# Seven products for eight in a quarter of the DeltaNet's v and z projections

## The chip, the cores and the metric

The kernel runs on one core of a Trainium2 chip, as one launch. The metric is the device time of that launch in microseconds, the median of several runs. TensorE multiplies matrices (its result lands in PSUM), VectorE (DVE in the profile) and ScalarE (ACT) do the elementwise work, GpSimd (POOL) some small work, and SyncE (SP) issues nearly all DMAs.

## The reference

Two decoder layers over 256 tokens of width 2048, all in float32: an attention layer (MLA) and a gated DeltaNet layer, each followed by a SwiGLU feed-forward and an embedding gate. The change is in the DeltaNet:

```python
proj = hn @ w_in                       # 256 x 2048 times 2048 x 12352
qkv, z, b, a = split(proj, ...)        # q 2048, k 2048, v 4096, z 4096, b 32, a 32 columns
qkv = silu(causal_depthwise_conv(qkv, conv_w))
...
o = chunk_gated_delta_rule(q, k, v, g, beta)     # from q, k, v; 32 heads
o = rms_norm(o, out_norm) * silu(z)
return o @ w_out
```

So z is needed late (when a head group's output is gated) and v when a head group is scanned, while q and k of all heads come first, because a triangular inverse over all heads is made from them.

## The kernel before

**Products.** Every float32 product is made of three TensorE passes on rounded operands: with x = xh + xl and w = wh + wl it sums xh·wh, xh·wl and xl·wh (lines 312 to 314, in `products`). Weights come in as raw tiles of four k-tiles by 512 columns (`wload`, a DMA of 1 MB on SyncE's queue) and are cut in two by `wsplit`: ScalarE casts `wh` (line 110), VectorE subtracts to get `wl` (line 111). There are 3 tiles each of `raw`, `wh` and `wl`, taken in turn; in the feed-forward stages `EXTRA` adds 3, 1 and 1.

**Plain projections.** `linear` takes blocks of 512 columns. A block is 16 k-tiles by two halves of 128 tokens by three passes, so 96 matmuls of 512 columns, which are summed in two PSUM banks and then copied out by the block's `evac`.

**Seven products for eight.** `seven` takes two column blocks at once. For part of the k-tiles it treats tokens, k and columns as a 2 x 2 by 2 x 2 block product and makes it with seven half-size products in place of eight (Strassen's scheme in Winograd's form). With `s` = 2 the first four k-tiles are treated so, in seven `phase`s of two k-tiles each (6 matmuls); the remaining k-tiles go as usual. The weight operands of those phases are sums and differences of raw blocks, made by VectorE in place (lines 344, 351, 358, 369), and each has to be split by `wsplit` again. The operands on the side of the tokens come from a `Half` object: eight transposes, `xf`, its split `xh`, `xl`, four sums `f`, and their split. `seven` waits for that object in its first phase: `op` calls `until`, which advances queued work until it is there. The feed-forward stages of both layers use `seven`, the DeltaNet does not.

**Queued work.** Work of another kind is written as generators in two lists, `fill` and `back`. `tick` advances the first generator of each list by one step, and `linear` and `seven` call it after every six matmuls. So the order in which instructions are written comes from these calls; a scheduler then settles each engine's order when the kernel is built, and each engine works through its own in that order.

**The DeltaNet stage.** First the four q and the four k projections, in pairs b = 0 to 3; `queries(b)` and `keys(b)` are queued behind them. `queries` convolves (`conv`: transposes, a scaled copy on ScalarE, twelve multiply-adds on VectorE, Silu) and sums squares with TensorE (`tr<-ones,sq`). `keys` convolves and then runs `group` for two head groups: products of `kap` and `rho` on TensorE, `dg`/`ssk` on VectorE, a power and a scaling of `E` on GpSimd, `LT` and `AT` on VectorE, then their stores. The eighth and last group is number 7. Behind q and k come eight z blocks, and after the first of them `fill` is emptied and `lanes` (62 small VectorE steps) is queued. One v block follows; then, with `scan(gg)` of eight head groups queued, the other seven v blocks and the output projection `w_out`.

The code that the change touches is this:

Of the kernel before, what the change touches and what calls it, by code (L numbers as in the profile page):

```python
# [11 lines left out]
F32R = mybir.dt.float32r  # L12
BF16 = mybir.dt.bfloat16
I32 = mybir.dt.int32
AF = mybir.ActivationFunctionType
# [5 lines left out]
P = 128  # L21
T = 2
# [16 lines left out]
Y2 = 3  # L39
S4 = 21  # L40
WBUFS = {"raw": 3, "wh": 3, "wl": 3}
EXTRA = {"raw": 3, "wh": 1, "wl": 1}
OGY = 5
PRE = 1
SY = 2
KY = 3
NV0 = 1
P2 = {"mla": 13, "gdn": 8, "ffn": 2, "ple": 2}


def cody_waite():
# [12 lines left out]
def trunk(ctx: ExitStack, tc: tile.TileContext, a: dict, out, plan=("mla", "ffn", "ple", "gdn", "ffn", "ple"), first=0):  # L64
# [25 lines left out]

    def wtile(kind, dt):

        more = EXTRA[kind] if scope.get("extra") is not None else 0
# [24 lines left out]
    nc.vector.memset(neghalf, -0.5)  # L118
    ones = const.tile([P, P], F32, name="ones")
    nc.vector.memset(ones, 1.0)  # L120

    def rsqrt_(t, n):
        nc.gpsimd.tensor_tensor(out=t, in0=t, in1=neghalf[:, :n], op=ALU.pow)  # L123
# [165 lines left out]
            assert fill or back  # L289
            tick()  # L290

    def linear(xs, W, kt, blocks, evac, row0=0, need=None, step=4):

        for bi, (c0, n) in enumerate(blocks):
            ps = [psmm.tile([P, 512], F32, tag="mm", name="mm") for _ in range(T)]
            for k4 in range(0, kt, 4):
                kn = min(4, kt - k4)
                raw = wload(W, row0 + k4 * P, c0, kn, n)
                wh, wl = wsplit(raw, kn, n, step)
                for kk in range(kn):  # L300
                    k = k4 + kk
                    if need is not None:
                        need(k // 4)
                    until(lambda: len(xs) > k // 4)
                    for t in range(T):
                        products(ps[t], part(xs, k, t), wh, wl, kk, n, k == 0, k == kt - 1)
                    tick()
            evac(bi, c0, n, ps)

# [467 lines left out]
    def gdn(j, nrm, nxt, mc, ctx):  # L777
# [88 lines left out]
        def project(c0):  # L866
# [7 lines left out]
            linear(nrm.x, W, 16, [(c0, 512)], evac)  # L874
            return xs

        def conv(acc, xs, f0):
            for pair in range(2):
                tr = trp()
                for k2 in range(2):  # L880
                    for t in range(T):
                        o = k2 * 256 + t * P
                        kk = pair * 2 + k2
                        nc.tensor.transpose(out=tr[:, o:o + P], in_=xs[:, t, kk * P:(kk + 1) * P], identity=ident)
                for k2 in range(2):
                    f = f0 + pair * 2 + k2
                    o = (pair * 2 + k2) * 256
                    src = tr[:, k2 * 256:(k2 + 1) * 256]
                    scaled(acc[:, o:o + 256], src, cw[:, 3 * 64 + f:3 * 64 + f + 1])
# [204 lines left out]
                yield from group(2 * b + i, rho, kap, Es[i])  # L1094

        lane_pool = tc.tile_pool(name="lane", bufs=1)
        with lane_pool as lp, tc.tile_pool(name="p2a", bufs=1) as scope["p2"]:
            for b in range(4):
                rho, Es = p4("rho"), []
                fill.append(queries(b, project(b * 512), rho, Es))  # L1100
                fill.append(keys(b, project(2048 + b * 512), rho, Es))
            for gg in range(8):
                linear(nrm.x, W, 16, [(8192 + gg * 512, 512 if gg < 7 else 256)],
                       lambda bi, c0, n, ps, gg=gg: gate_z(gg, 0, n, ps))
                if gg == 0:
                    while fill:
                        tick()
                    back.append(lanes(lp))
            first_v = [project(4096 + gg * 512) for gg in range(NV0)]
            while back:  # L1110
                tick()
        build = ctx.enter_context(tc.tile_pool(name="build", bufs=1))
        scope["p2"] = ctx.enter_context(tc.tile_pool(name="p2c", bufs=P2["gdn"]))
        tts = [build.tile([P, 8, P], F32, name=f"tt{i}") for i in range(2)]
        dd = build.tile([P, 8, 64], F32, name="dd")
        for z in (*tts, dd):
# [134 lines left out]
    for n, (s, i) in enumerate(steps):  # L1251
        last = n == len(steps) - 1
        nxt = None if last else Norm(WC[kind[steps[n + 1][0]], steps[n + 1][1]], {"ffn": 4}.get(steps[n + 1][0]))
        with ExitStack() as ctx:
            mc = ctx.enter_context(tc.tile_pool(name=f"{s}{n}", bufs=1))
            scope["extra"] = mc if s == "ffn" else None
# [41 lines left out]
```

## Time and profile before

| what | value |
|---|---|
| median of three runs | 2789.31 us (2788.46 to 2790.66) |
| the profiled execution's own time | 2787.68 us |
| span of its instructions | 2785.9 us |
| TensorE busy with matmuls | 2748.1 us, 13537 matmul records |
| VectorE busy | 2074.4 us |
| ScalarE busy | 1508.1 us |

The span is counted from the first to the last instruction of the profiled execution; 1.8 us of its time lie around it. Busy times of engines overlap, so they are not to be added. A matmul's recorded duration includes its way through the array and overlaps with the next one's; the distance between two starts says what a matmul costs in a row.

### The profile page before, as it was taken

The page shows a single profiled execution, that of the slowest core. Times are in us where ns is not written, and L with a number is a line of the kernel's source. Part 1 is how long each engine was busy: PE and PEld are TensorE (multiplying, and loading weights), DVE is VectorE, ACT ScalarE, POOL GpSimd, SP SyncE. Part 2 cuts the span into 40 slices and gives each one's busy share as a digit, 9 for nine tenths or more (in the row PEclk, how much of TensorE's full clock was granted, in tenths as well). Part 3 has the DMA queues.
Part 4 walks back from the last instruction along what each step waited for, and adds up shares of the span by engine and source line. Part 5 has one row for each costly group of instructions (what it writes and reads, how often), then busy time and mean ns, then how long its engine had stood idle before and what let it go on. Part 6 is the DMA issues. An engine that isn't in the chain of part 4 may idle for free.

```text
span 2785.9 us, 33751 instructions
## 1 busy us (share of the span) xinstructions
PE 2748.1 (99%) x13537; PEld 2281.5 (82%) x13537; DVE 2074.4 (74%) x1990; ACT 1508.1 (54%) x1625; POOL 170.5 (6%) x256
## 2 busy tenths in 40 slices
PE   8999999999999999999999999999999999999999
PEld 8888888888888888778888888888888888888887
DVE  5776888988978765566684556657898988989764
ACT  6765655655555555654444444444665655555553
POOL 1430000000000000233200000000000000000000
PEclk9999999999999999999999999999999999999999
DMA  7436465655566645666677545556565555655544
GB/s 226 129 119 206 150 240 181 226 172 201 186 211 212 221 134 174 215 218 225 225 263 248 198 156 188 165 172 217 181 215 192 186 193 182 239 205 204 192 155 141
DMA packets 296445, 540.81 MB, mean 194 GB/s; under 512 B 34105, under 2 KB 55266, under 8 KB 296034
## 3 DMA queue, kind: packets, MB, share of 16 engines
q1 hardware_dynamic: 295698, 536.52, 56.7%
q8 instruction: 106, 1.74, 0.3%
q10 hardware_dynamic: 592, 2.15, 0.2%
q14 instruction: 49, 0.40, 0.0%
HBM read 517.63 MB, written 21.00 MB: 193 GB/s over the span
## 4 chain that ended last, share of the span: by engine, by line
PE 89%; DVE 4%; ACT 3%; POOL 2%; issue 1%; DMA 1%; SPq 0%; DVEq 0%; POOLq 0%; ACTq 0%
PE mm L312 28%; PE mm L314 28%; PE mm L313 27%; DVE wl L111 2%; PE tr L156 1%; PE tr L1041 1%; ACT wh L110 1%; PE tr L1151 1%; PE tr L1157 1%; DMA E<-Gd 1%; POOL E L927 1%; ACT junk L178 1%; POOL r L123 0%; PE tr L944 0%; DVE kvs L582 0%
## 5 line engine op out<-in xcount | busy, mean ns | idle before, releaser
L111 DVE TENSOR_TENSOR wl<-raw,wh 128x2048 fp32r<-128x2048 f32 (+4 forms) x618 | 1265.2, 2062 | 436.7 <-ACT wh L110 435.6
L110 ACT CAST wh<-raw 128x2048 fp32r<-128x2048 f32 (+4 forms) x618 | 1059.2, 1725 | 832.8 <-PE mm L314 639.2
L312 PE MATMUL mm<-wh,xh 128*128 128x512 f32 (+3 forms) x3576 | 1407.8, 394 | 1.1 <-ACT xh L165 0.7
L314 PE MATMUL mm<-wh,xl 128*128 128x512 f32 (+3 forms) x3576 | 1385.2, 388 | 0.0
L313 PE MATMUL mm<-wl,xh 128*128 128x512 f32 (+3 forms) x3576 | 1383.0, 387 | 0.5 <-DVE wl L111 0.5
L314 PEld LDWEIGHTS mm<-wh,xl 128*128 128x128 f32 x3576 | 673.3, 188 | 137.4 <-DVE xl L654 0.2
L312 PEld LDWEIGHTS mm<-wh,xh 128*128 128x128 f32 x3576 | 674.3, 189 | 134.7 <-ACT u L354 3.8
L313 PEld LDWEIGHTS mm<-wl,xh 128*128 128x128 f32 x3576 | 674.5, 189 | 132.5 <-DVE wl L111 3.9
L123 POOL TENSOR_TENSOR re<-re,neghalf 128x2 f32<-128x2 f32 x2 | 5.4, 2722 | 1333.4 <-DVE re L748 1333.4
L344 DVE TENSOR_TENSOR raw<-raw 128x2048 f32<-128x2048 f32 (+1 forms) x34 | 65.0, 1911 | 14.2 <-DMA raw<-in_ffn_w_down 7.2
L702 ACT ACTIVATE sg<-mm,rs 128x512 f32<-128x512 f32 x44 | 30.4, 690 | 66.9 <-PE mm L314 66.9
L351 DVE TENSOR_TENSOR raw<-raw 128x2048 f32<-128x2048 f32 (+1 forms) x34 | 65.1, 1914 | 0.9
L358 DVE TENSOR_TENSOR raw<-raw 128x2048 f32<-128x2048 f32 (+1 forms) x34 | 65.0, 1912 | 0.7
L369 DVE TENSOR_TENSOR raw<-raw 128x2048 f32<-128x2048 f32 (+1 forms) x34 | 64.9, 1909 | 0.2
L165 ACT ACTIVATE xh<-tr,ncol 128x256 fp32r<-128x256 f32 x88 | 38.6, 476 | 19.8 <-PE tr L156 15.2
L166 DVE SCALAR_TENSOR_TENSOR xl<-tr,ncol,xh 128x256 fp32r<-128x256 f32 x88 | 39.3, 480 | 11.7 <-ACT xh L165 10.8
L446 DVE TENSOR_TENSOR h<-h,mm 128x512 f32<-128x512 f32 x56 | 37.1, 683 | 14.2 <-PE mm L314 14.2
L892 DVE SCALAR_TENSOR_TENSOR vT<-tr,cw,vT 128x255 f32<-128x255 f32 (+2 forms) x96 | 40.2, 475 | 9.7 <-ACT vT L439 9.5
L457 DVE TENSOR_TENSOR h<-h,mm 128x512 f32<-128x512 f32 x48 | 32.7, 683 | 13.4 <-PE mm L314 12.8
L312 PE MATMUL mm<-wh,x 128*128 128x512 f32 x88 | 34.5, 392 | 0.0
L314 PE MATMUL mm<-wh,x 128*128 128x512 f32 x88 | 34.4, 391 | 0.0
L313 PE MATMUL mm<-wl,x 128*128 128x512 f32 x88 | 34.3, 389 | 0.0
(298 smaller groups left out, 1726.2 us busy)
## 6 DMA issues: line engine op xcount, KB each, us to landing
raw<-in_ffn_w_gate_up SPq DMA_DIRECT2D x176, 1024.0 KB, 6.2
raw<-in_gdn_w_in SPq DMA_DIRECT2D x92, 1024.0 KB, 5.4
raw<-in_ffn_w_down SPq DMA_DIRECT2D x88, 1024.0 KB, 6.4
raw<-in_ple_w_gate SPq DMA_DIRECT2D x32, 1024.0 KB, 5.0
raw<-in_gdn_w_out SPq DMA_DIRECT2D x32, 1024.0 KB, 5.2
raw<-in_mla_w_o SPq DMA_DIRECT2D x16, 1024.0 KB, 5.1
raw<-in_mla_w_ukv SPq DMA_DIRECT2D x8, 1024.0 KB, 5.5
raw<-in_mla_w_in SPq DMA_DIRECT2D x8, 768.0 KB, 5.9
```

Source lines behind the costliest of these rows:

```text
L110: nc.scalar.copy(out=wh[:, k:e, :n], in_=src[:, k:e, :n])
L111: nc.vector.tensor_sub(out=wl[:, k:e, :n], in0=src[:, k:e, :n], in1=wh[:, k:e, :n].bitcast(F32))
L165: nc.scalar.activation(out=xh[:, s], in_=ps[:, c:c + n], func=AF.Copy, scale=w)
L166: nc.vector.scalar_tensor_tensor(out=xl[:, s], in0=ps[:, c:c + n], scalar=w, in1=xh[:, s].bitcast(F32), op0=ALU.mult, op1=ALU.subtract)
L312: mm(ps[:, :n], lhsT=xh, rhs=wh[:, kk, :n], start=start, stop=False, **kw)
L313: mm(ps[:, :n], lhsT=xh, rhs=wl[:, kk, :n], start=False, stop=False, **kw)
L314: mm(ps[:, :n], lhsT=xl, rhs=wh[:, kk, :n], start=False, stop=stop, **kw)
L344: nc.vector.tensor_sub(out=b12, in0=b12, in1=b11)
L351: nc.vector.tensor_sub(out=b12, in0=b22, in1=b12)
L358: nc.vector.tensor_sub(out=b11, in0=b12, in1=b11)
L369: nc.vector.tensor_sub(out=b21, in0=b21, in1=b12)
L892: nc.vector.scalar_tensor_tensor(out=acc[:, o + s:o + 256], in0=src[:, 0:256 - s], scalar=cw[:, jj * 64 + f:jj * 64 + f + 1], in1=acc[:, o ...
```

## The change

The v projections and six of the eight z blocks are made in pairs by `seven` with s = 2 (`project2`, `gates`), so that k-tiles 0 to 3 of 16 take seven products for eight. A `Half` of the first 512 columns of the normalised stream serves all of them; it is made by a generator `sums`, which is queued behind the last `keys`. In the DeltaNet a fourth raw weight tile is added, while `wh` and `wl` stay at three. z's blocks 6 and 7 go between v's second pair and the first output projection, and the first two v blocks are both made ahead. The half-wide z block gets two matmuls with a zero operand that clear its whole bank.

```diff
-EXTRA = {"raw": 3, "wh": 1, "wl": 1}
+EXTRA = {"ffn": {"raw": 3, "wh": 1, "wl": 1}, "gdn": {"raw": 1}}
...
+    zero = const.tile([P, P], F32R, name="zero")
+    nc.scalar.activation(out=zero, in_=ident, func=AF.Copy, scale=0.0)
...
+            if whole:
+                for t in range(T):
+                    mm(ps[t].rearrange("p (a c) -> p a c", a=4), lhsT=zero,
+                       rhs=zero.unsqueeze(1).to_broadcast([P, 4, P]), start=True, stop=False)
...
+        def sums():
+            yield
+            halfx.append(Half(lambda t: h[0][:, t, :], gain(nrm.wcol)))
+        def project2(c1, c2):
...
+            seven(nrm.x, of_half(lambda: halfx[0] if halfx else None), 2, W, 16, c1, c2, evac, u2col=nrm.rs[:, 0:1])
+            return xs
+        def gates(gg):
...
+            seven(nrm.x, of_half(lambda: halfx[0] if halfx else None), 2, W, 16, 8192 + gg * 512, 8704 + gg * 512, evac)
...
-        with lane_pool as lp, tc.tile_pool(name="p2a", bufs=1) as scope["p2"]:
+        with lane_pool as lp, tc.tile_pool(name="p2a", bufs=4) as scope["p2"]:
+            scope["extra"], scope["more"] = lp, EXTRA["gdn"]
             for b in range(4):
                 rho, Es = p4("rho"), []
                 fill.append(queries(b, project(b * 512), rho, Es))
                 fill.append(keys(b, project(2048 + b * 512), rho, Es))
-            for gg in range(8):
-                linear(nrm.x, W, 16, [(8192 + gg * 512, 512 if gg < 7 else 256)],
-                       lambda bi, c0, n, ps, gg=gg: gate_z(gg, 0, n, ps))
+            fill.append(sums())
+            for gg in (0, 2, 4):
+                gates(gg)
                 if gg == 0:
                     while fill:
                         tick()
                     back.append(lanes(lp))
-            first_v = [project(4096 + gg * 512) for gg in range(NV0)]
+            xv = project2(4096, 4608)
...
-        for gg in range(8):
-            fill.append(scan(gg, first_v[gg] if gg < NV0 else project(4096 + gg * 512)))
-            if gg in (3, 5):
-                w_out((gg - 3) // 2)
+        for i in range(4):
+            if i:
+                xv = project2(4096 + i * 1024, 4608 + i * 1024)
+            fill.extend(scan(2 * i + c, xv[c]) for c in range(2))
+            if i == 0:
+                continue
+            if i == 1:
+                for gg, n in ((6, 512), (7, 256)):
+                    linear(nrm.x, W, 16, [(8192 + gg * 512, n)], lambda bi, c0, n, ps, gg=gg: gate_z(gg, 0, n, ps), whole=n < 512)
+            if i < 3:
+                w_out(i - 1)
```

In the built order TensorE has 11088 weight matmuls (`mm<-`) before and 11048 after: 42 less for seven pairs, 2 more for the zero operand.

The first place is TensorE's order between the end of the last k projection and z. Before, 90 weight matmuls of the first z block stand between that projection and the sums of squares of `queries(3)`, the only others among them being two `tr<-ident,xs` of four; another 45 follow, and then these rows, which end with the last transposes of `keys(3)`:

```order
L944 MATMUL tr<-kap 128x128 x4
L944 MATMUL tr<-rho,kap 128x128 x4
L990 MATMUL tr<-ident,kap 128x128 x2
L944 MATMUL tr<-kap 128x128 x4
L944 MATMUL tr<-rho,kap 128x128 x4
L312 MATMUL mm<-wh,xh 128x512
L313 MATMUL mm<-wl,xh 128x512
L314 MATMUL mm<-wh,xl 128x512
L312 MATMUL mm<-wh,xh 128x512
L313 MATMUL mm<-wl,xh 128x512
L314 MATMUL mm<-wh,xl 128x512
L990 MATMUL tr<-ident,kap 128x128 x2
```

Of the change, TensorE's rows from the end of the same projection on are these; the last is the first matmul of z, in the first phase of `seven`, on the `xh` of the `Half`:

```order
L1031 MATMUL tr<-ident,kap 128x128 x2
L925 MATMUL tr<-ident,xs 128x128 x8
L949 MATMUL tr<-ones,sq 128x1 x8
L925 MATMUL tr<-ident,xs 128x128 x8
L985 MATMUL tr<-kap 128x128 x4
L985 MATMUL tr<-rho,kap 128x128 x4
L1031 MATMUL tr<-ident,kap 128x128 x2
L985 MATMUL tr<-kap 128x128 x4
L985 MATMUL tr<-rho,kap 128x128 x4
L1031 MATMUL tr<-ident,kap 128x128 x2
L402 MATMUL tr<-ident,h_86 128x128 x8
L318 MATMUL mm<-wh,xh 128x512
```

All of `queries(3)`, `keys(3)` and the transposes of the `Half` now stand in one piece, and the 141 weight matmuls that stood among them stand behind.

The second place is VectorE at the end of the same work, from group 6's `LT` on. Before:

```order
L971 TENSOR_TENSOR LT<-tr,E 128x1024
L971 TENSOR_TENSOR AT<-tr,E 128x1024
L950 SCALAR_TENSOR_TENSOR dg,ssk<-tr,ident 128x128 x4
L954 TENSOR_SCALAR ssk<-ssk 128x4
L111 TENSOR_TENSOR wl<-raw,wh 128x2048
L971 TENSOR_TENSOR LT<-tr,E 128x1024
L971 TENSOR_TENSOR AT<-tr,E 128x1024
L111 TENSOR_TENSOR wl<-raw,wh 128x2048 x2
```

And of the change:

```order
L1012 TENSOR_TENSOR LT<-tr,E 128x1024
L1012 TENSOR_TENSOR AT<-tr,E 128x1024
L991 SCALAR_TENSOR_TENSOR dg,ssk<-tr,ident 128x128 x3
L995 TENSOR_SCALAR ssk<-ssk 128x4
L1012 TENSOR_TENSOR LT<-tr,E 128x1024
L1012 TENSOR_TENSOR AT<-tr,E 128x1024
L429 TENSOR_TENSOR xl<-xf,xh 128x1024
L418 TENSOR_TENSOR f<-xf 128x256
L420 TENSOR_TENSOR f<-xf 128x256
L419 TENSOR_TENSOR f<-f,xf 128x256
L421 TENSOR_TENSOR f<-xf,f 128x256
L429 TENSOR_TENSOR xl<-f,xh 128x1024
```

The six rows of the `Half` stand behind the last group's `AT`, and the splits for z's later phases behind them. Between group 5's `LT` and the first multiply-add of `queries(3)` stood its `AT` and one split of four k-tiles; now there stand a split of two k-tiles, the `AT` and the raw differences of lines 357 and 364.

Elsewhere in the q and k projections the order is almost the same. The sums of squares of `queries(1)` stand 23 weight matmuls earlier on TensorE, and on VectorE one split of four k-tiles stands behind its multiply-adds instead of before them.

## Rows read from the trace of the kernel before

**Rows 1.** The page: busy times of the engines, and the chain that ended last, by engine.

```profile
PE 2748.1 (99%) x13537; PEld 2281.5 (82%) x13537; DVE 2074.4 (74%) x1990; ACT 1508.1 (54%) x1625; POOL 170.5 (6%) x256
...
PE 89%; DVE 4%; ACT 3%; POOL 2%; issue 1%; DMA 1%; SPq 0%; DVEq 0%; POOLq 0%; ACTq 0%
```

**Rows 2.** Windows: busy times PE, PEld, DVE, ACT, POOL; granted clock, DMA share, GB/s.

```profile
224.00:920.00 696.00, 695.21 (x3091) 569.19 (x3090) 594.63 (x396) 397.07 (x327) 0.73 (x1) 1.00 0.57 198
...
1161.90:1165.40 3.50, 3.50 (x9) 2.76 (x10) 2.37 (x2) 0.00 (x0) 3.10 (x1) 0.50 1.00 321
```

**Rows 3.** Timeline of TensorE around its wait in queries(0): start, us, instruction.

```profile
1154.84 0.39 PE L313 MATMUL mm<-wl,xh 128*128 128x512 f32 x1
1155.07 0.39 PE L314 MATMUL mm<-wh,xl 128*128 128x512 f32 x1
1158.58 3.44 PE L908 MATMUL tr<-ones,sq 128*128 128x1 f32 x16 [3.12 <-ACT sq L903]
1161.87 0.77 PE L312 MATMUL mm<-wh,xh 128*128 128x512 f32 x1
...
1165.01 0.63 PE L313 MATMUL mm<-wl,xh 128*128 128x512 f32 x1
```

**Rows 4.** Timeline of TensorE from the last k projection's end: the small matmuls alone.

```profile
1329.89 0.38 PE L990 MATMUL tr<-ident,kap 128*128 128x128 f32 x2
...
1351.77 1.95 PE L908 MATMUL tr<-ones,sq 128*128 128x1 f32 x16
1353.57 1.07 PE L884 MATMUL tr<-ident,xs 128*128 128x128 f32 x8
1364.72 1.05 PE L944 MATMUL tr<-kap 128*128 128x128 f32 x8
...
1372.31 0.44 PE L990 MATMUL tr<-ident,kap 128*128 128x128 f32 x2 [2.15 <-DVE LT L971]
```

**Rows 5.** Timeline of VectorE in the same stretch: start, us, instruction.

```profile
1333.12 1.23 DVE L971 TENSOR_TENSOR LT<-tr,E 128x1024 f32<-128x1024 f32 x1 [3.69 <-POOL E L961]
1334.26 1.22 DVE L971 TENSOR_TENSOR AT<-tr,E 128x1024 f32<-128x1024 f32 x1
...
1341.22 2.42 DVE L892 SCALAR_TENSOR_TENSOR rho<-tr,cw,rho 128x255 f32<-128x255 f32 x6
...
1371.02 1.23 DVE L971 TENSOR_TENSOR LT<-tr,E 128x1024 f32<-128x1024 f32 x1 [3.71 <-POOL E L961]
...
1381.24 1.21 DVE L971 TENSOR_TENSOR AT<-tr,E 128x1024 f32<-128x1024 f32 x1
```

**Rows 6.** Timeline of ScalarE in the same stretch.

```profile
1350.65 1.06 ACT L903 ACTIVATE sq<-rho 128x1024 f32<-128x1024 f32 x1
1354.24 0.91 ACT L439 ACTIVATE kap<-tr,cw 128x256 f32<-128x256 f32 x2 [2.53 <-PE tr L884]
...
1363.33 1.06 ACT L897 ACTIVATE kap<-kap 128x1024 f32<-128x1024 f32 x1
```

**Rows 7.** Timeline of GpSimd in the same stretch: one step in groups 6 and 7.

```profile
1368.51 0.20 POOL L957 TENSOR_TENSOR k<-rk 128x4 f32<-128x4 f32 x1
...
1375.96 1.82 POOL L957 TENSOR_TENSOR k<-rk 128x4 f32<-128x4 f32 x1
```

**Rows 8.** Groups by shape over the whole run, VectorE: xcount, busy, mean ns, idle.

```profile
L111 DVE TENSOR_TENSOR wl<-raw,wh 128x1024 fp32r<-128x1024 f32 x96 | 117.5, 1224 | 86.7 <-ACT wh L110 86.7
...
L361 DVE TENSOR_TENSOR mm<-mm,m 128x512 f32<-128x512 f32 x34 | 23.6, 693 | 0.6 <-PE mm L314 0.3
...
L351 DVE TENSOR_TENSOR raw<-raw 128x1024 f32<-128x1024 f32 x12 | 14.7, 1225 | 0.4
...
L423 DVE TENSOR_TENSOR xl<-xf,xh 128x1024 fp32r<-128x1024 f32 x8 | 9.8, 1220 | 5.9 <-ACT xh L422 5.9
...
L415 DVE TENSOR_TENSOR f<-xf,f 128x256 f32<-128x256 f32 x6 | 2.5, 419 | 0.0
```

**Rows 9.** Groups by shape in a feed-forward down projection, 390 to 436 us, TensorE.

```profile
L312 PE MATMUL mm<-wh,xh 128*128 128x512 f32 x66 | 26.0, 395 | 0.0
...
L313 PE MATMUL mm<-wl,xh 128*128 128x512 f32 x66 | 25.7, 390 | 0.0
```

**Rows 10.** Timeline of TensorE: the sums of squares of queries(1), small matmuls alone.

```profile
1228.68 1.95 PE L908 MATMUL tr<-ones,sq 128*128 128x1 f32 x16
```

More of the change, by code (lines that the diff above doesn't have):

```diff
@@ L46 @@
 KY = 3
-NV0 = 1
-P2 = {"mla": 13, "gdn": 8, "ffn": 2, "ple": 2}
+P2 = {"mla": 13, "gdn": 9, "ffn": 2, "ple": 2}
 def cody_waite():
@@ L91, in wtile @@
     def wtile(kind, dt):
-        more = EXTRA[kind] if scope.get("extra") is not None else 0
+        more = scope["more"].get(kind, 0)
         i = turn[kind] % (WBUFS[kind] + more)
@@ L290, in until, with linear @@
             tick()
-    def linear(xs, W, kt, blocks, evac, row0=0, need=None, step=4):
+    def linear(xs, W, kt, blocks, evac, row0=0, need=None, step=4, whole=False):
         for bi, (c0, n) in enumerate(blocks):
             ps = [psmm.tile([P, 512], F32, tag="mm", name="mm") for _ in range(T)]
+            if whole:
+                for t in range(T):
+                    mm(ps[t].rearrange("p (a c) -> p a c", a=4), lhsT=zero,
+                       rhs=zero.unsqueeze(1).to_broadcast([P, 4, P]), start=True, stop=False)
             for k4 in range(0, kt, 4):
@@ L305, in linear @@
                     for t in range(T):
-                        products(ps[t], part(xs, k, t), wh, wl, kk, n, k == 0, k == kt - 1)
+                        products(ps[t], part(xs, k, t), wh, wl, kk, n, k == 0 and not whole, k == kt - 1)
                     tick()
@@ L875, in project, with evac @@
             return xs
+        halfx = []
+        def sums():
+            yield
+            halfx.append(Half(lambda t: h[0][:, t, :], gain(nrm.wcol)))
+        def project2(c1, c2):
+            xs = [p4("xs").rearrange("p (t n) -> p t n", t=T) for _ in range(2)]
+            def evac(c, t, ps, u2):
+                if u2 is None:
+                    scaled(xs[c][:, t, :], ps, nrm.rs[:, t:t + 1])
+                else:
+                    nc.vector.scalar_tensor_tensor(out=xs[c][:, t, :], in0=ps, scalar=nrm.rs[:, t:t + 1], in1=u2,
+                                                   op0=ALU.mult, op1=ALU.add)
+            seven(nrm.x, of_half(lambda: halfx[0] if halfx else None), 2, W, 16, c1, c2, evac, u2col=nrm.rs[:, 0:1])
+            return xs
+        def gates(gg):
+            sz = [p4("sz").rearrange("p (t n) -> p t n", t=T) for _ in range(2)]
+            def evac(c, t, ps, u2):
+                z = sz[c][:, t, :]
+                if u2 is not None:
+                    nc.vector.tensor_add(out=z, in0=ps, in1=u2)
+                    ps = z
+                nc.scalar.activation(out=z, in_=ps, func=AF.Silu, scale=nrm.rs[:, t:t + 1])
+                if (c, t) in ((0, 0), (1, 1)):
+                    nc.sync.dma_start(out=Zd[gg + c], in_=sz[c])
+            seven(nrm.x, of_half(lambda: halfx[0] if halfx else None), 2, W, 16, 8192 + gg * 512, 8704 + gg * 512, evac)
         def conv(acc, xs, f0):
@@ L1108, in gdn @@
                     back.append(lanes(lp))
-            first_v = [project(4096 + gg * 512) for gg in range(NV0)]
+            xv = project2(4096, 4608)
             while back:
                 tick()
+        scope["extra"] = None
         build = ctx.enter_context(tc.tile_pool(name="build", bufs=1))
         scope["p2"] = ctx.enter_context(tc.tile_pool(name="p2c", bufs=P2["gdn"]))
+        scope["extra"] = build
         tts = [build.tile([P, 8, P], F32, name=f"tt{i}") for i in range(2)]
@@ L1255, in trunk @@
             mc = ctx.enter_context(tc.tile_pool(name=f"{s}{n}", bufs=1))
-            scope["extra"] = mc if s == "ffn" else None
+            scope["extra"], scope["more"] = mc, EXTRA.get(s, {}) if s != "gdn" else {}
             if s != "gdn":
```

## The prediction

> **What bounds the kernel now.** The page comes first: TensorE is busy for 2748.1 of 2785.9 us, and 89% of the chain that ended last is TensorE [rows 1]. So the kernel is a row of matmuls, and only two things change its time: how many there are, and how long TensorE stands. The price of one is the distance between two starts in the timeline, 1155.07 - 1154.84 = 0.23 us for 512 columns; read over longer stretches it is 0.227 (the 141 matmuls counted below fit it). The recorded 0.39 us of one overlaps with the next [rows 3]. The same timeline shows what a wait costs: from 1155.07 to 1158.58 TensorE stands for ScalarE's squares, and then runs at the lower level of its clock, 1.2 GHz, a granted 0.50 [rows 2]: the sums of squares take 3.29 us (1158.58 to 1161.87) where they take 1.80 at 1351.77, and the next eight weight matmuls lie 0.45 us apart (1161.87 to 1165.01 in seven steps) [rows 3, 4].
>
> **What is taken away.** Seven pairs save two products of four k-tiles' halves each, six matmuls a pair, 42 in all; the zero operand adds 2. 40 x 0.227 = 9.1 us less.
> The Trainium skill (TensorE: Matmul & The Clock Gate, section Back-to-back issue gap) gives about 131 ns as the sustained spacing of 512-column matmuls that each come with a weight load; by it the 40 would be worth 5.2 us. The row has 0.23 us for just such pairs, and the measurement decides.
>
> **The hole.** The gain needs the Half before the first phase of the first z pair, and the Half is queued behind all of queries(3) and keys(3). In TensorE's new order nothing but the 46 small matmuls of that work and 8 transposes of the Half stand between the last k projection and z; the 141 weight matmuls that stood among them (32.0 us at 0.227) now stand behind. TensorE takes its matmuls in the written order: in queries(0) it stood for 3.5 us though the weights behind were split for matmuls that ran right after [rows 3].
> The Trainium skill (PSUM — Partial Sum Buffer, section Engine vs sequencer instructions) states that matmuls start and complete in program order. By that rule the hole is open and costs what follows; if matmuls could overtake, nothing but the 9.1 us would be left. The trace's wait agrees with the rule.
>
> How long the hole is follows from the chain, on the clock of before. The last k projection ends at 1329.89, where two transposes follow it [rows 4].
> - VectorE has group 5's LT at 1333.12; it waits for GpSimd then, so nothing new is ahead of it. Behind it now come one split of two k-tiles, AT and two raw differences, all of 1024 elements and 1.14 us apart (1333.12 to 1334.26) [rows 5]; the first multiply-add of queries(3) starts at 1334.26 + 4 x 1.14 = 1338.8.
> - Six multiply-adds 2.42 (the row at 1341.22), one split 1.14, six more 2.42: 1344.8 [rows 5].
> - Silu and squares, 1.06 each: 1346.9 [rows 6].
> - Sums of squares. TensorE has stood nearly idle for 15 us, where a stand of 3.5 us was enough for the lower level, so 3.29 and not 1.80: 1350.2 [rows 3, 4].
> - The k convolution: its first four transposes 0.9 (half of 1.07, at the lower level twice that), scaled copy 0.5, six multiply-adds 2.42, copy 0.5, six more 2.42, Silu 1.06: 1358.0 [rows 4 to 6].
> - Groups 6 and 7. Before, from Silu's end (1363.33 + 1.06 = 1364.39) to the end of the last AT (1381.24 + 1.21) passed 18.1 us [rows 5, 6]. One GpSimd step took 1.82 there instead of 0.20 [rows 7], and the weight split between is gone from the order: 15.5 at least. Slower matmuls add about 1. I take 17: 1375.0.
> - The Half: split 1.22, four sums at 0.42, a cast (1.06, as ScalarE's other rows of 1024 elements), split 1.22 [rows 6, 8]: 5.2, so 1380.2. By then the eight matmuls that need less can have run (1.8 us), so it is as if TensorE started again at 1378.4.
>
> That is 48.5 us. The small matmuls that before has too are in it: its stretch from 1329.89 to 1372.31 is 42.4 us, less 32.0 of weight matmuls and 2.15 of waiting [rows 4], leaves 8.2. 48.5 - 8.2 = 40.3 us idle, less the 2.15 that before lost there too: 38.2. Eight matmuls at the lower level after it, 0.22 more each: 1.8. **The hole costs 40.0 us.** Its lower bound takes 1.80 for the sums, 15.5 for the groups, no loss of clock and a convolution start that gains 1 or 2 more from the freed engines: 32. Its upper one lets the chain run as slowly as before, when the weight work was among it: last AT at 1382.45, so 47.
>
> **The other sums of squares.** Those of queries(1) started at 1228.68 without waiting [rows 10], and now stand 23 x 0.227 = 5.2 us earlier. VectorE's multiply-adds ahead of them gain one split of four k-tiles, about 2.2 us (twice a step of 1.14). So TensorE would stand for up to 3.0 us, with some loss of clock as in queries(0): 0 to 7, and I take 3.5, about one such stand.
>
> **Seven splits for four.** A pair's first six phases last 36 x 0.227 = 8.2 us on TensorE. VectorE needs for them six splits of 1.22, three differences of 1.22 and one sum of 0.69: 11.7 [rows 8]. The 3.5 us too many must have been worked ahead, and with three wh and wl tiles only two can be ahead when the last phase of the pair before is still reading the third. In the down projection of the feed-forward the same seven run with one tile more of each and TensorE never waits [rows 9], so 0 is the lower bound; 3.5 for each of the six pairs behind the first, 21, is the upper one. One tile less is one split of 1.22 not worked ahead; I take 1.5 a pair, 9 us.
>
> **At nothing.** On average VectorE has room: it is busy for 595 of 696 us in the feed-forward stages, where TensorE has no hole (695.2 busy) [rows 2]. The raw loads behind the load of `lanes` on SyncE's queue wait for the last group's stores, but the first of them is needed only by the 91st weight matmul of z, 20 us after TensorE starts again. The fourth raw tile, the p2 slots and ScalarE's added casts (one for each split, at most as long as VectorE's) lie beside the splits already counted. z's blocks 6 and 7 keep their matmuls, and give the queued scans 32 steps of cover where the seven pairs take away a few; I see no price for it. If these covers failed, it would be inside the 21 us above.
>
> **The sum**, against the profiled execution's own time: 2787.68 - 9.1 + 40.0 + 3.5 + 9 = 2831.1 us. The median of the three runs is 1.6 us above that execution, well inside the range. From no change this kernel's runs can be told at about 0.2%, 5.6 us.
>
> **The rivals.**
> - *The engines, freed of the weight work, run the chain much faster*, and the sevens do not starve: -9.1 + 32 = +23 or less, 2805 to 2811. For it: VectorE and ScalarE have nothing else to do in the hole. Against: nearly every step above is a serial row of this trace, and GpSimd's wait (3.69 and 3.71 before LT) was not caused by weight work [rows 5]. Chance 0.12.
> - *VectorE becomes the bound of every pair*: the upper 21 us, and the hole: 2843, with the upper hole 2850. For it: the order puts steps of `lanes` and of the scans between the splits. Against: [rows 9]. Chance 0.12.
> - *Faster*: the hole closes, because its steps are done while the k projection still runs, and only the 9.1 us remain: 2779. The place is the row of transposes between the k projection and z; the point that decides is a hole under 9.1 us. For it: the feed-forward's Half is ready long before its use and TensorE does not wait [rows 9]. Against: the last convolution needs the projection that ends at 1329.89, and from there twelve multiply-adds and two groups are still to come. Chance 0.04; no difference 0.02.
>
> **How the numbers follow.** The forecast has 0.70: 2831, its own range 2815 to 2845. The range that should hold the time 8 times in 10 reaches from 2812 (a hole of 33 with no starving pair) to 2850 (a hole of 45, and most of the starving). Faster by over 0.2%: 0.04; within: 0.02; slower: 0.94.
>
> **What the changed profile would show.** Right: on TensorE's timeline, between the last `tr<-ones,sq` and z's first `mm`, some 40 us with only small matmuls, waits put down to VectorE and ScalarE, a granted clock near 0.5 there, and weight matmuls 0.43 to 0.45 apart just behind; a few short waits for `wl` in the first six phases of each pair; a new wait ahead of the second `tr<-ones,sq`. Wrong: weight matmuls within that stretch, a last AT that ends less than 35 us after the k projection, or pairs in which TensorE stands for over 3 us each. Then the group's chain or the number of split tiles was misread.

## The result and the profile after

The changed kernel took 2850.63 us (median of 5 runs, 2849.11 to 2854.83) against 2789.31 us before: a ratio of 1.0222, 95% interval 1.0211 to 1.0233. It is slower by 61 us where 42 were forecast (2831 against 2789.3), and it ends 0.6 us above the range. The profiled run took 2849.11 us; its span is 2846.8 us.

The page of the changed kernel, its span, TensorE's row of busy times, and TensorE's busy share and granted clock in 40 slices of 71 us:

```profile
span 2846.8 us, 33884 instructions
...
PE 2764.0 (97%) x13505; PEld 2283.5 (80%) x13505; DVE 2145.7 (75%) x2073; ACT 1541.5 (54%) x1684; POOL 169.5 (6%) x256
...
PE   8999999999999999997899999999999999999999
...
PEclk9999999999999999998999999999999999999999
```

TensorE was busy for 99% of the span [rows 1] and is for 97%. Only the 19th and 20th slices, 1281 to 1423 us, show it; the rest of the loss is too thin for this view.

The hole, in TensorE's timeline from the end of the last k projection to z (small matmuls and the first five of z):

```profile
1325.22 0.39 PE L1031 MATMUL tr<-ident,kap 128*128 128x128 f32 x2
1325.44 1.04 PE L925 MATMUL tr<-ident,xs 128*128 128x128 f32 x8
1336.62 3.57 PE L949 MATMUL tr<-ones,sq 128*128 128x1 f32 x16 [10.15 <-ACT sq L944]
1340.06 1.95 PE L925 MATMUL tr<-ident,xs 128*128 128x128 f32 x8
1348.18 2.08 PE L985 MATMUL tr<-kap 128*128 128x128 f32 x8 [6.17 <-ACT kap L938]
...
1356.79 0.44 PE L1031 MATMUL tr<-ident,kap 128*128 128x128 f32 x2 [2.74 <-DVE LT L1012]
1357.69 1.09 PE L402 MATMUL tr<-ident,h 128*128 128x128 f32 x8 [0.46 <-ACT k L1033]
1361.08 0.80 PE L318 MATMUL mm<-wh,xh 128*128 128x512 f32 x1 [2.30 <-ACT xh L428]
1361.67 0.63 PE L319 MATMUL mm<-wl,xh 128*128 128x512 f32 x1
1366.16 0.80 PE L320 MATMUL mm<-wh,xl 128*128 128x512 f32 x1 [3.86 <-DVE xl L429]
1366.75 0.63 PE L318 MATMUL mm<-wh,xh 128*128 128x512 f32 x1
```

These rows answer to [rows 4]. From 1325.44 to 1361.08 no weight matmul runs, and each step waits for VectorE or ScalarE. The windows view of this stretch (columns as in [rows 2]) shows TensorE busy for 15.5 of 41 us, with a granted clock of 0.66, between the two levels:

```profile
1325.00:1366.00 41.00, 15.48 (x82) 13.36 (x80) 24.05 (x53) 12.32 (x22) 9.24 (x15) 0.66 0.24 79
```

**Where the 61 us went.** TensorE is the bound, so its losses can be added from its timeline: from each matmul's start to the next one's, less 0.227 us for 512 columns, or less the median distance of its own shape for a small one. The stretches are cut by counting weight matmuls from the start: the DeltaNet begins behind 4488, the k projections end with 5352, a pair has 192 or 186. In us, from the profiled execution of each kernel (the runs are the experiments below):

| stretch | before | after | run 1 | run 2 | run 3 | run 5 | run 6 | run 7 | run 8 | run 12 |
|---|---|---|---|---|---|---|---|---|---|---|
| ahead of the DeltaNet | 31.7 | 32.7 | 32.2 | 29.8 | 32.6 | 30.8 | 29.6 | 30.6 | 31.9 | 30.2 |
| its q and k | 18.0 | 12.3 | 12.1 | 11.5 | 11.7 | 8.6 | 10.6 | 8.9 | 12.4 | 11.1 |
| z's first pair, with the hole | 3.0 | 37.7 | 13.6 | 37.2 | 38.0 | 39.7 | 5.1 | 5.1 | 4.4 | 0.7 |
| the next four pairs of blocks | 1.0 | 20.7 | 25.4 | 4.3 | 21.1 | 21.0 | 12.3 | 13.4 | 1.0 | 6.4 |
| on to the last quarter of `w_out` | 16.4 | 19.6 | 22.4 | 16.2 | 24.7 | 22.5 | 17.9 | 18.7 | 18.1 | 19.8 |
| the last quarter | 0.0 | 7.3 | 7.1 | 7.3 | 0.1 | 7.5 | 7.2 | 0.0 | 0.0 | 0.0 |
| the feed-forward's first 280 | 0.5 | 9.9 | 9.9 | 8.7 | 8.6 | 5.6 | 8.6 | 0.5 | 0.5 | 0.5 |
| the rest | 6.3 | 6.1 | 6.2 | 5.1 | 6.2 | 6.1 | 5.1 | 5.2 | 6.2 | 5.1 |
| sum | 76.9 | 146.2 | 129.0 | 120.1 | 143.0 | 141.8 | 96.5 | 82.4 | 74.5 | 73.8 |

After less before: 69.3 us lost, less 9.1 for 40 matmuls, is 60.2; the spans differ by 60.9. So nothing large is outside this table. Its first two rows differ by up to 4 us between kernels that have the same code there, which is the grain of single profiles.

### The profile page after: what moved, and what is told of

It reads as the page before. It is cut to its first block, busy times and chain, and to the rows that moved or that the text cites. A ratio compares the mean times of both kernels' runs of the same rounds, so it can differ in the third digit from the quotient of the medians.

```text
span 2846.8 us, 33884 instructions
## 1 busy us (share of the span) xinstructions
PE 2764.0 (97%) x13505; PEld 2283.5 (80%) x13505; DVE 2145.7 (75%) x2073; ACT 1541.5 (54%) x1684; POOL 169.5 (6%) x256
## 4 chain that ended last, share of the span: by engine, by line
PE 45%; DVE 3%; ACT 1%; issue 1%; DMA 0%; POOL 0%; DVEq 0%; ACTq 0%
PE mm L318 14%; PE mm L319 14%; PE mm L320 14%; DVE wl L110 1%; PE tr L1082 1%; PE tr L1195 1%; ACT wh L109 1%; PE tr L1201 1%; PE tr L157 1%; DMA raw<-in_gdn_w_in 0%; POOL r8o L124 0%; PE tr L1176 0%; PE tr L925 0%; DVE vb L1254 0%; DVE pr L1050 0%
## 5 line engine op out<-in xcount | busy, mean ns | idle before, releaser
L110 DVE TENSOR_TENSOR wl<-raw,wh 128x2048 fp32r<-128x2048 f32 (+3 forms) x653 | 1292.6, 1996 | 393.4 <-ACT wh L109 392.2
L109 ACT CAST wh<-raw 128x2048 fp32r<-128x2048 f32 (+3 forms) x653 | 1082.2, 1670 | 804.8 <-PE mm L320 641.1
L350 DVE TENSOR_TENSOR raw<-raw 128x2048 f32<-128x2048 f32 (+1 forms) x41 | 73.6, 1794 | 19.1 <-DMA raw<-in_gdn_w_in 7.8
L357 DVE TENSOR_TENSOR raw<-raw 128x2048 f32<-128x2048 f32 (+1 forms) x41 | 73.6, 1795 | 0.9
L364 DVE TENSOR_TENSOR raw<-raw 128x2048 f32<-128x2048 f32 (+1 forms) x41 | 73.6, 1795 | 0.8
L375 DVE TENSOR_TENSOR raw<-raw 128x2048 f32<-128x2048 f32 (+1 forms) x41 | 73.4, 1791 | 0.2
L445 ACT ACTIVATE xs<-mm,rs 128x512 f32<-128x512 f32 x28 | 18.9, 688 | 44.6 <-PE mm L320 44.6
L463 DVE TENSOR_TENSOR h<-h,mm 128x512 f32<-128x512 f32 x48 | 32.7, 683 | 13.4 <-PE mm L320 12.8
L353 ACT COPY mm<-mm 128x512 f32<-128x512 f32 x41 | 23.5, 572 | 22.7 <-PE mm L320 22.7
L318 PE MATMUL mm<-wh,x 128*128 128x512 f32 x88 | 34.5, 392 | 0.0
```

The lines of the kernel that those rows point to most:

```text
L109: nc.scalar.copy(out=wh[:, k:e, :n], in_=src[:, k:e, :n])
L110: nc.vector.tensor_sub(out=wl[:, k:e, :n], in0=src[:, k:e, :n], in1=wh[:, k:e, :n].bitcast(F32))
L318: mm(ps[:, :n], lhsT=xh, rhs=wh[:, kk, :n], start=start, stop=False, **kw)
L350: nc.vector.tensor_sub(out=b12, in0=b12, in1=b11)
L357: nc.vector.tensor_sub(out=b12, in0=b22, in1=b12)
L364: nc.vector.tensor_sub(out=b11, in0=b12, in1=b11)
```

## The experiments

The twelve runs were taken beside the kernel before, whose medians there lay between 2789.1 and 2789.6 us.

**Run 1: the Half earlier.** `sums` is queued ahead of `queries(3)`.

```diff
             for b in range(4):
+                if b == 3:
+                    fill.append(sums())
...
-            fill.append(sums())
             for gg in (0, 2, 4):
```

> The changed kernel, but the step that makes the Half of h[0] is queued ahead of queries(3) instead of behind keys(3), so that the first seven-product pair of z needs nothing that is still queued, and the small matmuls of queries(3) and keys(3) stand among its weight matmuls again. Theory A (the hole is a term of its own, read from the changed kernel's trace as about 33 us more idle than before had there): 2850.6 - 33 = 2818, between 2812 and 2823. Rival B (the hole only shows where the time is lost; queries(3) and keys(3) need VectorE and ScalarE, which the splits of the sevens keep busy, so most of the loss comes back as stands within the z pairs): 2835 or more.

2827.62 us, 1.0134 [1.0117, 1.0151]: 23 us less, between the two theories. The hole shrinks by 24 us, but 13.6 are left in the first pair, and its longest waits say why:

```profile
PE mm L318 <- ACT xh L428: 4.5, 2, 2.4
PE mm L318 <- ACT wh L109: 1.0, 1, 1.0
PE tr L949 <- ACT sq L944: 0.8, 1, 0.8
```

(Sum of the waits, their number, the longest; 1320 to 1392 us.) `xh` is still the Half's own: it was made while z had already begun.

**Run 2: split tiles shared.** Two fast splits of two k-tiles share one `wh` and one `wl` tile of four.

```diff
+        def cut2(src):
+            if s == 4:
+                return wsplit(src, s)
+            if not halves:
+                w = wtile("wh", F32R), wtile("wl", F32R)
+                halves.extend((w[0][:, i:i + 2], w[1][:, i:i + 2]) for i in (0, 2))
+            wh, wl = halves.pop(0)
...
-        phase(A, fast("A11"), wsplit(b11, s), s, True)
+        phase(A, fast("A11"), cut2(b11), s, True)
```

> The changed kernel, but two fast splits of two k-tiles each share one wh tile and one wl tile of four (first half, second half), so that the seven splits of a pair take four tiles of each ring and not seven. Theory A (the pairs starve because a split must wait for a tile that is still read, so the count of tiles is the limit): most of the about 20 us that the z pairs lose comes back, 2828 to 2838. Rival B (VectorE's 11.7 us of work for 8.2 us of matmuls is the limit, whatever the number of tiles): 2846 to 2852.

2825.20 us, 1.0129 [1.0114, 1.0144]: 25 us less, and the number of tiles was the limit: by the table 16.4 of the 25 lie in the four pairs behind the first, and 3.4 in the stretch with the other two. (The edit also holds for the feed-forward's pairs of that kind; the first row has 2.9 less, about the grain.) TensorE's three longest waits, 1376 to 1640 us in the changed kernel, which takes in the four pairs:

```profile
PE mm L319 <- DVE wl L110: 7.5, 8, 1.8
PE mm L318 <- ACT wh L109: 2.9, 5, 1.3
PE mm L318 <- DVE mm L367: 1.5, 2, 0.9
```

and the one wait that is left with shared tiles, 1376 to 1610 us:

```profile
PE mm L319 <- DVE wl L110: 0.2, 1, 0.2
```

The windows of z's second and third pair and v's first, of the changed kernel and then of run 2, show that VectorE's work is the same:

```profile
1414.00:1554.00 140.00, 131.74 (x558) 104.72 (x557) 112.72 (x119) 70.70 (x61) 2.31 (x3) 0.99 0.66 227
```

```profile
1409.50:1537.80 128.30, 127.87 (x559) 104.37 (x558) 111.77 (x120) 70.67 (x61) 2.31 (x3) 1.00 0.70 240
```

VectorE does 112 us in both, in 140 or in 128: it had room, and was kept from working ahead.

**Run 3: the second quarter of `w_out` behind the fourth v pair.**

```diff
-            if i < 3:
-                w_out(i - 1)
+            if i == 1:
+                w_out(0)
+        w_out(1)
         w_out(2)
```

> The changed kernel, but the second quarter of the output projection stands behind the fourth v pair instead of ahead of it, so that the last two scans have 64 k-tile steps of cover instead of 32 ahead of the last quarter. Theory A (the stands of about 17 us around the last quarter and at the start of the feed-forward come from the last scan, which is drained in one piece there): 2831 to 2836. Rival B (only the stand of 3.6 us and the clock after it belong to the scan, and the later ones, about 9 us at the start of the feed-forward, come from the rings of split tiles, which arrive there in another turn): 2843 to 2847.

2847.29 us, 1.0208 [1.0193, 1.0223]: 3.3 us less. The scan's stand is gone (last quarter 7.3 to 0.1), but two v pairs now follow each other directly and the stretch with them loses 5.1 more, and the feed-forward keeps 8.6, no less than in runs 2 and 6, which leave the scan in its place. The time is Rival B's; run 5 shows that B's cause for the feed-forward's stands is at most a part.

**Run 4: the queued work run out ahead of z, in the kernel before.**

```diff
+            while fill:
+                tick()
             for gg in range(8):
```

> The kernel before, with one edit: what is queued of queries(3) and keys(3) is run out ahead of z's first block, so that their small matmuls stand together on TensorE with no weight matmuls among them. No product is changed. Theory A (the hole costs the same without the sevens): 2789.3 + 30 to 36, so 2819 to 2826; the Half is not in it, about 5 us less than the first estimate of 40. Rival B (the hole is long in the changed kernel only because the raw differences and the Half's sums stand in it): 2789.3 + 22 or less, so 2811 or less.

2792.80 us, 1.0012 [1.0003, 1.0022]: both theories missed, since no hole came about. TensorE's small matmuls from the last k projection's end (the rows between them, left out, are weight matmuls):

```profile
1329.06 0.60 PE L884 MATMUL tr<-ident,xs 128*128 128x128 f32 x4
...
1333.34 0.66 PE L884 MATMUL tr<-ident,xs 128*128 128x128 f32 x4 [2.31 <-DVE LT L971]
...
1349.32 1.95 PE L908 MATMUL tr<-ones,sq 128*128 128x1 f32 x16
```

The scheduler put z's weight matmuls among them, although they were written behind. (The engine itself does not mix: ahead of 1333.34 it stood for 2.31 us, although the split of the weights behind had ended at 1326.96, and they ran at once after. The Trainium skill (PSUM — Partial Sum Buffer, section Engine vs sequencer instructions) has matmuls in program order; the row agrees.) So the run prices no hole, but it shows what makes one: not the order in which the code is written, but that z's first matmuls need the Half.

**Run 5: three raw tiles for `w_out`.** The fourth is given up when the last v pair is through.

```diff
+            if i == 3:
+                scope["more"] = {}
```

> The changed kernel, but the fourth raw tile is given up behind the last v pair: the output projection's weights go round three raw tiles again. Theory A (the feed-forward's three additional raw tiles lie in memory of which the DeltaNet's fourth raw tile has a part; their first loads wait until the last weight of the output projection is split, at 2019.8 in the changed kernel's trace, where before they were issued at 1933 to 1943; this makes the stands of about 9 us at the feed-forward's start): 2850.6 - 8.5, between 2840 and 2844. Rival B (these stands come from the rings of split tiles or from the last scan, which is late): 2849 to 2852.

2846.92 us, 1.0202 [1.0185, 1.0219]: 3.7 us less, half of what was expected. The feed-forward's start loses 5.6 instead of 9.9. The queue's timeline of the feed-forward's first weight loads explains runs 3 and 5 together. Changed kernel, run 3, run 5, and run 7, which has both edits:

```profile
1981.24 0.37 SPq L101 DMA_DIRECT2D raw<-in_gdn_w_out  x1
1996.15 25.20 SPq L101 DMA_DIRECT2D raw<-in_ffn_w_gate_up  x6
```

```profile
1997.89 21.50 SPq L101 DMA_DIRECT2D raw<-in_ffn_w_gate_up  x6
```

```profile
1999.97 23.64 SPq L101 DMA_DIRECT2D raw<-in_ffn_w_gate_up  x6
```

```profile
1929.78 0.92 SPq L101 DMA_DIRECT2D raw<-in_ffn_w_gate_up  x2
```

In run 7 the first loads go out at 1929.8, 47 us ahead of the feed-forward's first weight matmul; before they went out 46 ahead of it. In the other three they start at 1996 to 2000, 31 to 35 ahead. Two things hold the loads, each for about as long: the last scan, which ends late (in run 5 the first load goes out right behind `xl` of line 167, the scan's last step, which ends at 1999.91), and the fourth raw tile, which still holds a weight of `w_out` (in run 3 the first load goes out at the end of that weight's split, at 1997.87). Taking away one leaves the other.

**Run 6: shared split tiles, and the Half ahead of `queries(2)`** (the edits of runs 1 and 2, with `b == 2`).

> The changed kernel with the shared split tiles of the second run, and with the step that makes the Half queued ahead of queries(2), one block earlier than in the first run. Theory A (what was left in the first z pair of the first run, 13 us, came from a Half that was still made only when the pair had begun, and from seven splits that needed seven tiles): the hole's 35 us go in full, 2825.2 - 35 = 2790, between 2786 and 2794. Rival B (VectorE cannot do queries(3), keys(3) and the splits of the first pairs at once): 2800 or more.

2801.21 us, 1.0040 [1.0025, 1.0054]: 24 us below run 2, and Rival B's time. The hole is gone (5.1), but the pairs behind it lose 12.3 where run 2 lost 4.3: steps of `keys(3)` now stand between their splits on VectorE. VectorE is not full there, which Rival B asks for: the longest of the three waits on `wl` (1320 to 1480 us) is for a split that stands behind the last group's `LT`, and `LT` waits for GpSimd:

```profile
PE mm L319 <- DVE wl L110: 6.1, 3, 4.0
```

```profile
1385.75 1.22 DVE L1025 TENSOR_TENSOR LT<-tr,E 128x1024 f32<-128x1024 f32 x1 [3.68 <-POOL E L1015]
1386.89 1.21 DVE L1025 TENSOR_TENSOR AT<-tr,E 128x1024 f32<-128x1024 f32 x1
1388.02 2.28 DVE L110 TENSOR_TENSOR wl<-raw,wh 128x2048 fp32r<-128x2048 f32 x1
```

**Run 7: all four edits** (runs 3, 5 and 6 together).

> All four edits together: the Half ahead of queries(2), shared split tiles, the fourth raw tile given up behind the last v pair, and the second quarter of the output projection behind the fourth v pair. Theory A (the terms add: 2790 as in the run above, less 8.5 for the feed-forward's loads, less 7 for the scan that was drained ahead of the last quarter): 2775, between 2770 and 2780, faster than the kernel before by 9 to 19 us. Rival B (the removed stands come up again elsewhere, as the move of the quarter alone showed: 8.5 us gone, 5 us come back): 2783 to 2792.

2784.69 us, 0.9983 [0.9974, 0.9992]: 4.7 below the kernel before, short of the 9 to 19 of theory A, and a time of Rival B's. But the stands did not come up elsewhere: run 7 is 16.5 us below run 6, where theory A had 15.5 for the two edits; run 6, from which they were counted, had itself come out 11 us above its own theory A. The last quarter and the feed-forward's start lose 0.5 together, as before; the pairs still lose 13.4.

**Run 8: four p2 tiles in the kernel before.**

```diff
-        with lane_pool as lp, tc.tile_pool(name="p2a", bufs=1) as scope["p2"]:
+        with lane_pool as lp, tc.tile_pool(name="p2a", bufs=4) as scope["p2"]:
```

> The kernel before with one number changed: four p2 tiles instead of one in the queries and keys stage. Theory A (with one tile, the copy of the diagonal waits until the k tile that went out of the same buffer has left by DMA, which holds the next group back: the stands at 1243.29 and 1284.91 before, 5.3 us, are this wait): 2789.3 - 5.5, between 2782 and 2786. Rival B (the stage's gain of 5.7 us in the changed kernel comes from the fourth raw tile, or from the move of the two v blocks): 2788 to 2791.

2784.38 us, 0.9985 [0.9976, 0.9995]: 5.0 us less from this number alone (three of its ten runs lie at 2789, like the kernel before). Theory A has the size. TensorE's waits in q and k name ScalarE's rows. Before, 1060 to 1330 us:

```profile
PE tr L908 <- ACT sq L903: 4.6, 2, 3.1
PE tr L944 <- ACT kap L897: 3.5, 2, 3.1
```

and in run 8, 1060 to 1326 us:

```profile
PE tr L908 <- ACT sq L903: 3.5, 1, 3.5
PE tr L944 <- ACT kap L897: 2.0, 2, 1.7
```

The two stands that the expectation names, 3.11 and 1.46 us at TensorE, are down to 0.28 and 0.07; two others grow by 0.4 and 1.3. And VectorE's rows bear out the mechanism up to them: the second group of a pair starts with `dg`, which takes a p2 tile, as the first group's `k` did. Before, group 5's `dg` stands behind the landing of group 4's `k` (at 1325.27):

```profile
1321.46 0.74 SPq L993 DMA_DIRECT2D KQd<-k  x1
1327.93 0.28 DVE L950 SCALAR_TENSOR_TENSOR dg<-tr,ident 128x128 f32<-128x128 f32 x1
```

In run 8 it starts ahead of that landing (at 1320.06), and `LT` follows it by 5.2 us in both:

```profile
1316.25 0.74 SPq L993 DMA_DIRECT2D KQd<-k  x1
1316.60 0.28 DVE L950 SCALAR_TENSOR_TENSOR dg<-tr,ident 128x128 f32<-128x128 f32 x1
1321.78 1.22 DVE L971 TENSOR_TENSOR LT<-tr,E 128x1024 f32<-128x1024 f32 x1 [3.69 <-POOL E L961]
```

Groups 1 and 3 show the same. Whether `dg` waited there or was placed there by the scheduler is not shown.

**Run 9: z's plain blocks first.** z's blocks 6 and 7 stand ahead of z's pairs, the Half ahead of `queries(3)`, the quarters as v, v, v, first, v, second, third, fourth; shared split tiles, three raw tiles at the end.

> z's two plain blocks stand ahead of z's three pairs again, directly behind the k projections, so that queries(3) and keys(3) have plain weight matmuls around them and the pairs have VectorE to themselves; with it the Half ahead of queries(3), shared split tiles, the fourth raw tile given up behind the last v pair, and the quarters of the output projection placed as v, v, v, first quarter, v, second, third, fourth. Theory A (the 13 us that the kernel with all four edits lost in the first z pairs are splits and convolution steps that share VectorE; placed apart they cost nothing, and the whole saving of products is left beside the gain of the four p2 tiles): 2784.4 - 9.1 = 2775, between 2771 and 2779. Rival B (the pairs lose the time by themselves, whatever stands beside them): 2782 to 2787.

2792.60 us, 1.0010 [1.0002, 1.0019]: worse than run 7; theory A fails. Block 7 is half as wide, 0.120 us a matmul, so the two blocks' 194 matmuls last only 33.8 us, 42.0 with the small matmuls among them (1321.73 to 1363.75). The work of `queries(3)` and `keys(3)` among weight work lasts longer (to 1382.45 before, 52.6 from the last k projection [rows 4, 5]). What is left stands in the first pair:

```profile
1366.36 0.39 PE L320 MATMUL mm<-wh,xl 128*128 128x512 f32 x1
1372.23 0.69 PE L1044 MATMUL tr<-ident,kap 128*128 128x128 f32 x2 [5.48 <-DVE LT L1025]
```

That is not what makes it slower than run 7, though. Counted as in the table, its first five pairs of blocks lose 17 us, where run 7 loses 18.5; but from there on to the last quarter it loses 26 us and run 7 19. Of the 26, 13 lie in the last v pair.

**Run 10: that move alone, in the changed kernel**: z's blocks 6 and 7 ahead of z's pairs, the Half as in the change.

> The changed kernel with one edit: z's two plain blocks stand ahead of z's three pairs, directly behind the k projections, instead of among the v pairs. Theory A (the hole is only want of matmuls that do not need the Half, and shrinks from 35 us to the Half's own steps, about 5; but the scans lose 32 steps of cover, so that the first quarter of the output projection comes when 31 of some 46 steps of scans 0 and 1 are through, and the other 15, at about 1 us each, are a new hole there): 2850.6 - 30 + 15 = 2836, between 2828 and 2842. Rival B (the place of z's two blocks among the v pairs has no price, as the prediction put it): 2816 to 2823.

2841.81 us, 1.0187 [1.0171, 1.0203]: at the upper end of theory A's range (2836, to 2842), and Rival B is out. The small matmuls run among plain weights, but the hole goes only to the Half's own steps, and the first quarter of `w_out` stands for a scan without cover. Counted as in the table, the stretch with the scan loses 15 us more than in the change, as theory A had it; what is left of the hole costs some 17 us and not 5, since the Half's `xl` stands in VectorE's order behind the last group's `LT`, which waits 3.68 us for GpSimd:

```profile
1372.00 0.63 PE L319 MATMUL mm<-wl,xh 128*128 128x512 f32 x1
1380.65 0.79 PE L320 MATMUL mm<-wh,xl 128*128 128x512 f32 x1 [8.01 <-DVE xl L429]
```

```profile
1673.04 1.96 PE L157 MATMUL tr<-ident,vb 128*128 128x128 f32 x7 [5.84 <-DVE vb L1255]
```

**Runs 11 and 12: plain z blocks ahead of the pairs.** Run 7 with z's blocks 0 to 5 plain (run 11), or 0 to 3 plain and 4, 5 as a pair (run 12), and the queued work run out behind the second block.

```diff
-            for gg in (0, 2, 4):
-                gates(gg)
-                if gg == 0:
+            for gg in range(4):
+                linear(nrm.x, W, 16, [(8192 + gg * 512, 512)], lambda bi, c0, n, ps, gg=gg: gate_z(gg, 0, n, ps))
+                if gg == 1:
...
+            for gg in (4,):
+                gates(gg)
```

> The kernel with all four edits, but z's first six blocks are plain again (24 weight matmuls fewer than the kernel before, 2 zero ones more), and the queued work of queries(3) and keys(3) is run out behind z's second block. What is left of the change: seven products in the four v pairs. Theory A (the loss of the four-edit kernel sits in the z pairs that share VectorE with queries(3) and keys(3); the v pairs keep what they save): 2784.4 of the four p2 tiles alone, less 22 x 0.227 = 5.0, less up to 3 of the wait that the later run-out saves: 2776 to 2781. Rival B (VectorE loses in the v pairs, to the scans, what they save): 2783 to 2787.

> The same, but z's blocks 4 and 5 are a seven-product pair, behind four plain blocks (30 weight matmuls fewer than before, 2 zero ones more). Theory A (a z pair that no convolution stands beside keeps its 6 x 0.227 = 1.4 us): 1 to 2 us below the kernel with plain z blocks, 2775 to 2780. Rival B (the pair pays for itself in stands, the lanes' steps on VectorE being beside it): equal to that kernel or above it.

Run 11: 2778.51 us, 0.9962 [0.9949, 0.9974]. Run 12: 2778.18 us, 0.9958 [0.9945, 0.9972]. Run 11 is as theory A has it, though it loses 3.9 us at the feed-forward's start, counted as in the table, where runs 7 and 12 lose 0.5; run 12's pair can't be told from plain blocks. Both are faster than the kernel before by 11 us and than the changed one by 72. All of TensorE's waits in run 12, 1320 to 1480 us, where the changed kernel has its hole and run 7 lost 13 us:

```profile
PE mm L319 <- DVE wl L110: 1.9, 2, 1.1
PE mm L319 <- DVE wl L358: 0.6, 1, 0.6
```

## Why the prediction was wrong

The direction and the main cause were right; the sum of +43.4 us was 18 short. Two terms came out larger, the splits by 14 (22.9 for 9, scans included) and the covers put at nothing by 16.7; two came out smaller, the hole by 5.3 and the q and k stage by 9.2. That the time ends only 0.6 us above the range is luck: without the two smaller ones it would lie some 15 above. Term by term, by the table:

- **Products.** -9.1 holds: with it the table closes within 0.7 us. The time shows it between runs 8 and 12, which lose about the same (74.5 and 73.8): 28 matmuls less, 6.4 us, and 6.2 us measured.
- **The hole.** 40.0 forecast, 32 to 47 as bounds; 37.7 - 3.0 = 34.7 measured. The chain was as worked out from the sums of squares on: from `kap`'s Silu (ended at 1348.13) to the end of the last `AT` (1364.98) passed 16.9 us, where 17 was taken. Ahead of it the first multiply-add of `queries(3)` started 3.2 us behind the last k projection, not 8.9. VectorE's rows, of which `LT` answers to the first of [rows 5]:

```profile
1322.58 1.22 DVE L1012 TENSOR_TENSOR LT<-tr,E 128x1024 f32<-128x1024 f32 x1 [3.68 <-POOL E L1002]
...
1328.38 2.42 DVE L933 SCALAR_TENSOR_TENSOR rho<-tr,cw,rho 128x255 f32<-128x255 f32 x6
...
1363.76 1.22 DVE L1012 TENSOR_TENSOR AT<-tr,E 128x1024 f32<-128x1024 f32 x1
```

  Group 5's `LT` came 2.6 us ahead of the last k projection's end, and 3.2 behind it in the kernel before. The four p2 tiles alone do this: in run 8 it comes 2.9 ahead. (Another order of the splits moves it too: in run 2, with the four tiles, it comes 1.6 behind.) A small slip in the sum: the four transposes taken as 0.9 are 1.07 by the prediction's own words.
- **Sums of squares of queries(1).** +3.5 forecast; they did not wait (1224.88, no idle time before them). The whole q and k stage gained 5.7, since the p2 tiles, which the prediction put among the things at nothing, are worth 5.0 (run 8).
- **Seven splits for four.** 9 forecast for six pairs, 21 as the upper bound; 20.7 - 1.0 = 19.7 for the four pairs behind the first, and 3.2 in the stretch with the other two, scans included. The mechanism is shown by run 2, which takes 16.4 of the 20.7, but the sum's 1.5 a pair was mis-sized: it measures 4.9 (2.8 to 7.1), above the 3.5 that the bound was made from. The prediction named stands of over 3 us a pair as the sign that the number of split tiles was misread, and the sign came: three tiles were read rightly, and what they cost was not.
- **At nothing.** This is the step that failed: "z's blocks 6 and 7 keep their matmuls, and give the queued scans 32 steps of cover where the seven pairs take away a few; I see no price for it." The last quarter and the feed-forward's start lose 17.2 us instead of 0.5: 16.7, and without it the time would have lain in the range, at 2834. Nor is it inside the 21 us of the pairs, where the prediction put it if the covers failed: the pairs took 20 of those themselves. There are two causes, and runs 6 and 7, which differ by the edits against them alone (those of runs 3 and 5), lie 16.5 us apart. The last two scans are queued together behind the fourth v pair, with 32 k-tile steps ahead of the last quarter; in the kernel before, `scan(6)` had the 16 steps of v's last block as well. Run 3 takes that stand away. And the fourth raw tile, costed at nothing too, holds up the feed-forward's loads together with the late scan (runs 3, 5 and 7). The prediction asked of z's blocks what they give, not which steps stand last.
- **The rival by which the engines, freed, run the chain much faster** was near in the hole (34.7 against 32), and wrong in its condition that the sevens do not starve. **VectorE as the bound of every pair** has the size but not the cause: run 2 leaves VectorE its work and takes most of the loss.

What stays open: how a later `dg` comes to TensorE's waits for ScalarE in q and k, which go with it in run 8, and why run 11 loses 3.9 us at the feed-forward's start though its first loads go out 47 us ahead, as in run 7. The two edits of runs 3 and 5 were not run together without those of run 6.

## What to carry to other kernels

Look for what the first instruction of the new scheme needs, and for what can run until it is there: a scheduler will mix independent work in (run 4), but not work that waits for the operand (the change; run 1 gives the operand earlier and gets 24 us of the hole back). Price each removed piece of cover by the last steps that it covered, and a tile added to a pool also by who takes its memory next. Where an edit brings more, smaller pieces through a ring of buffers, let two share one buffer before adding buffers: here that gave 25 us of the 61 back.

## What the runs showed of the hardware

In the hole the mean granted clock was 0.66 over 41 us, and the first weight matmuls behind it lay 0.43 us apart (1366.75 to 1367.18), 0.23 again from 1372.6 on. At the feed-forward's start two waits in parallel hid each other: of 9.9 us lost, 5.6 are left without the fourth raw tile (run 5), 8.6 with the scan moved (run 3, and no less than in runs 2 and 6, which move neither), and 0.5 with both (run 7). In the q and k stage `LT` of groups 1, 3 and 5 waits 3.68 or 3.69 us for GpSimd's `E`, in the kernel before, in the change and in run 8 alike.
